# Four subtractions per weight block, on GpSimd instead of VectorE, in a decoder-block kernel that TensorE fills

## The chip, the cores and the metric

The kernel runs on one core of one Trainium2 chip. The core has a matrix engine (TensorE, in the profile PE, with its weight loads as PEld), a vector engine (VectorE, DVE), an activation engine (ScalarE, ACT), a general-purpose engine (GpSimd, POOL), an engine that only issues transfers here (SyncE, SP), and sixteen DMA engines. Each engine works through its own queue of instructions in order; semaphores tie the queues together. The metric is the device time in microseconds of one execution, of which the median over several runs is given.

## The reference: what is computed

One decoder layer on a sequence of 256 tokens with a model width of 2048, all in float32. Cut to its matrix products:

```python
proj = x @ w_in                      # 2048 -> q/k/v/gates of two attention branches, merge gates
...                                  # gated linear attention, forgetting attention
merged = sigmoid(ma) * (o @ w_branch_gla) + sigmoid(mb) * (of @ w_branch_fox)
x = layer_norm(ALPHA * x + merged @ w_out)
h = gelu(causal_dwconv(x @ w_gate)) * (x @ w_up)     # 2048 -> 5632, twice
x = layer_norm(ALPHA * x + h @ w_down)               # 5632 -> 2048
x = x + sigmoid(x @ w_ple_gate) * (p @ w_ple_proj)
```

The weights are read once each; nearly all the time goes into these products.

## The kernel before, in words

**Units of weights.** The weights lie in memory as a list of units, each 128 partitions by 2048 float32 (1 MB). Every unit is loaded by two transfers on SP's queue into two tiles `raw` of 128x1024, taken from a ring of five. TensorE multiplies in a rounded float32, so every operand is split in two: ScalarE writes the rounded value `hi` (a copy, line 113), VectorE the remainder `lo` = raw - hi (line 227 for plain units, line 195 for the units of this case). Both have rings of six tiles of 128x1024. A product is then three matmuls: hi by hi, lo by hi, hi by lo.

**Units with seven block products.** For `gv`, `gr`, `wo` and `dn` (the value projection, its output gate, the output projection and the down projection) a unit is a 2x2 set of blocks b11, b12, b21, b22 of 128x512. A plain ("classic") unit takes eight block products, 24 matmuls. In 33 chosen units (`s_units`) the Strassen-Winograd scheme takes seven, 21 matmuls, for which four differences of weight blocks are needed beside b11, b21 and b22:

t1 = b12 - b11, t3 = b12 - b22, t2 = b22 - t1, t4 = b21 - t2.

The function `differences` makes them in place, two per call. I call the four subtractions sub1 to sub4, in the order t1, t3, t2, t4. `prep_s` prepares such a unit: it splits b11 (tiles `hi_b`, `lo_b`), then b22 and b21 together, then overwrites b11 and b12 with t1 and t3 and splits these (`hi_t`, `lo_t`), then overwrites b22 and b21 with t2 and t4 and splits these. A subtraction that overwrites a block must come after the split that reads it: sub1 after the `lo_b` of b11, sub3 after the `lo_b` of b22 and b21. So a unit takes four `hi` and four `lo` tiles, in a chain that runs to and fro between ScalarE and VectorE. TensorE uses the seven products in a fixed order: b11, b21, b22 first, then t1, t3, t2, and t4 last (b11, t1, t3 and t2 accumulate in tiles named `dn_p`, `gv_p` and so on, the others in `dn`, `gv`).

**Parked units.** For 13 of the 33 units the differences are made long before, in an earlier stage (`park_gen`): the unit is loaded into a tile `td` of 128x2048, the four subtractions run, and GpSimd's queue stores the result to a DRAM tensor (line 165), from where `prep_s` reads it back. The other 20 subtract in the stage itself, on the tiles `raw`. Altogether there are 132 subtractions of 128x512, 52 on `td` and 80 on `raw`.

**What sets the order.** A function `unit` prepares three units ahead of the one in use (`ahead=3`); how far the preparation can really run ahead is set by the rings of `raw`, `hi` and `lo`. SP's queue is in the order of the program. The other queues are put in order by a scheduler that goes by priorities and expected costs when the kernel is built. In the stages `gv`, `gr`, `wo` and `dn` seven-product units mostly alternate with classic ones. GpSimd has little to do: it issues some accumulating loads (line 223), the stores of `td`, `sd` and others, and in the gate/up stage it copies two columns per block into `gp` for the convolution (line 1295), which VectorE's instructions of line 1302 read.

Of the kernel before, what the change touches and what calls it, by code (L numbers as in the profile page):

```python
# [14 lines left out]
ALU = mybir.AluOpType  # L15
# [58 lines left out]
def tile_block(ctx: ExitStack, tc: tile.TileContext, wu, wfv, wpp, xT_in, x_in, pT_in, wlr,  # L74
               chan, gnorm, lng, ident_in, mask_in, cmask_in, out):
    nc = tc.nc
# [69 lines left out]

    def differences(r0, r1, h):
        b12, b11, b22, b21 = r0[:, 0:512], r0[:, 512:1024], r1[:, 0:512], r1[:, 512:1024]
        sub = lambda o, a, b: nc.vector.tensor_tensor(o, a, b, ALU.subtract)  # L149
        if h == 0:  # L150
            sub(b11, b12, b11)
            sub(b12, b12, b22)
        else:
            sub(b22, b22, b11)
            sub(b21, b21, b22)

    def park_gen(units):

        for u, i in [(u, i) for u, i in parked.items() if u in units]:
            w = s8([P, 2048], name=f"td{i}")  # L160
            nc.sync.dma_start(w, wu[u])
            yield
            for h in range(2):
                differences(w[:, 0:1024], w[:, 1024:2048], h)
            nc.gpsimd.dma_start(td[i], w)
            yield

    def prep_s(u):
# [31 lines left out]
        if u not in parked:  # L200
            differences(r0, r1, 0)
        t3, t1_ = split(rt[0], "t13")
        if u not in parked:
            differences(r0, r1, 1)
# [240 lines left out]
    for u in range(8):  # L445
        hi, lo = fvu[u]
        for j in range(2):
            kt = 2 * u + j
            a = xT[kt // 4][:, kt % 4, :]
# [6 lines left out]
            for t, i, c in seq:  # L456
                o, n = fch[c]
# [1124 lines left out]
```

## Time and profile before

| | us |
|---|---|
| runs of the kernel before (three) | 1662.21, 1662.29, 1662.49 |
| profiled execution, first to last instruction (span) | 1660.7 |
| PE busy | 1654.7 |
| DVE busy | 1214.7 |
| ACT busy | 938.7 |
| POOL busy | 112.1 |

The profiled execution is known by its span; the median of the runs is 1.6 us above it, which is what lies before the first and after the last instruction. The page of the profile gives busy time per engine, the chain of work that ended last, and groups of instructions by line. Other views give the waits between engines, and the instructions of one engine in order of time. In that last view a row has the start, the duration, the engine, the line, the operation, the tiles written and read, their shapes, how many instructions were merged, and in brackets the idle time before it and what ended it. The durations of matmuls include their way through the pipeline; the pace is read from their starts.

### The profile page before, as it was taken

The numbers are of one execution on the slowest core, as the hardware profiler recorded it, in microseconds if no ns is written. First come the engines' busy times: TensorE is split into PE (matmuls) and PEld (weight loads), VectorE is DVE, ScalarE is ACT, GpSimd is POOL, SyncE is SP. The second block draws the span as 40 slices with busy tenths as digits, with TensorE's granted clock in tenths as the row PEclk, the third lists the DMA queues.
The fourth block names the chain that finished last, engine by engine and source line by source line (L and its number), as shares of the span: only waits on it lengthen the run. The fifth ranks groups of instructions, "written<-read, shape, count | busy, mean of one in ns | idle before, by whom it ended". The sixth has DMA issues, their size and how long they took to land.

```text
span 1660.7 us, 24379 instructions
## 1 busy us (share of the span) xinstructions
PE 1654.7 (100%) x8935; PEld 1438.0 (87%) x8935; DVE 1214.7 (73%) x1869; ACT 938.7 (57%) x1355; POOL 112.1 (7%) x262
## 2 busy tenths in 40 slices
PE   9999999999999999999999999999999999999999
PEld 8988888888888888888898888888888888888887
DVE  7644655678876547888987777877777787998774
ACT  6766666765555754455575445555545555556543
POOL 0111111100000110000010010000000000000000
PEclk9999999999999999999999999999999999999999
DMA  8799999986676997878856687777777668798554
GB/s 321 253 253 243 258 263 260 266 233 201 203 224 183 246 251 278 304 247 301 313 175 203 206 291 266 254 240 248 255 250 254 204 227 322 276 359 319 179 187 158
DMA packets 110313, 414.16 MB, mean 249 GB/s; under 512 B 12473, under 2 KB 13761, under 8 KB 104049
## 3 DMA queue, kind: packets, MB, share of 16 engines
q1 hardware_dynamic: 97584, 359.11, 62.7%
q0 software_dynamic: 12608, 53.49, 13.6%
q8 instruction: 70, 1.15, 0.3%
q14 instruction: 51, 0.41, 0.1%
HBM read 388.43 MB, written 24.13 MB: 248 GB/s over the span
## 4 chain that ended last, share of the span: by engine, by line
PE 98%; DMA 1%; DVE 0%; ACT 0%; POOL 0%; SPq 0%; issue 0%; POOLq 0%
PE dn L799 11%; PE psu L294 10%; PE psg L294 9%; PE psm L294 7%; PE pg L340 5%; PE psu L296 5%; PE psg L296 5%; PE gv L799 4%; PE wo L799 4%; PE psm L296 4%; PE psa L294 4%; PE dn_p L799 3%; PE gr L340 3%; PE fv L459 2%; PE gr L799 2%; PE psa L296 2%
## 5 line engine op out<-in xcount | busy, mean ns | idle before, releaser
L113 ACT ACTIVATE hi<-raw 128x1024 fp32r<-128x1024 f32 x502 | 528.2, 1057 | 405.1 <-issue 139.2
L227 DVE TENSOR_TENSOR lo<-raw,hi 128x1024 fp32r<-128x1024 f32 x444 | 539.7, 1222 | 214.9 <-ACT hi L113 210.8
L294 PE MATMUL psu<-x1T,hi 128*128 128x512 f32 x688 | 240.5, 392 | 0.0
L294 PE MATMUL psg<-x1T,hi 128*128 128x512 f32 x672 | 234.9, 392 | 0.0
L296 PE MATMUL psu<-x1T,lo 128*128 128x256 f32 x688 | 192.5, 280 | 0.0
L296 PE MATMUL psg<-x1T,lo 128*128 128x256 f32 x672 | 188.0, 280 | 0.0
L294 PE MATMUL psm<-xT,hi 128*128 128x512 f32 x512 | 181.2, 397 | 0.0
L294 PEld LDWEIGHTS psu<-x1T,hi 128*128 128x128 f32 x688 | 129.3, 188 | 27.4
L294 PEld LDWEIGHTS psg<-x1T,hi 128*128 128x128 f32 x672 | 126.2, 188 | 26.8
L296 PE MATMUL psm<-xT,lo 128*128 128x256 f32 x512 | 143.4, 280 | 0.0
L296 PEld LDWEIGHTS psu<-x1T,lo 128*128 128x128 f32 x688 | 130.7, 190 | 0.0
L296 PEld LDWEIGHTS psg<-x1T,lo 128*128 128x128 f32 x672 | 127.7, 190 | 0.0
L294 PEld LDWEIGHTS psm<-xT,hi 128*128 128x128 f32 x512 | 96.3, 188 | 19.6
L799 PE MATMUL dn<-hi,hC 128*128 128x512 f32 x400 | 111.4, 390 | 0.0
L296 PEld LDWEIGHTS psm<-xT,lo 128*128 128x128 f32 x512 | 97.3, 190 | 0.1
L294 PE MATMUL psa<-oT,hi 128*128 128x512 f32 x256 | 89.5, 392 | 0.0
L799 PEld LDWEIGHTS dn<-hi,hC 128*128 128x128 f32 x400 | 75.1, 188 | 15.5
L113 ACT ACTIVATE hi_t<-raw 128x1024 fp32r<-128x1024 f32 x40 | 42.5, 1062 | 65.7 <-DVE raw L149 51.1
L113 ACT ACTIVATE hi_b<-raw 128x512 fp32r<-128x512 f32 x66 | 55.2, 841 | 42.7 <-DMA raw<-in_wu_dram 19.9
L223 POOL DMA_DIRECT2D lo<-in_wu_dram x58 | 51.0, 879 | 320.9 <-ACT lo L113 125.6
L296 PE MATMUL psa<-oT,lo 128*128 128x256 f32 x256 | 71.6, 280 | 0.0
L195 DVE TENSOR_TENSOR lo_b<-raw,hi_b 128x512 fp32r<-128x512 f32 x66 | 62.5, 954 | 11.4 <-ACT hi_b L113 11.4
(374 smaller groups left out, 3254.5 us busy)
## 6 DMA issues: line engine op xcount, KB each, us to landing
raw<-in_wu_dram SPq DMA_DIRECT2D x555, 512.0 KB, 5.7
lo<-in_wu_dram POOLq DMA_DIRECT2D x58, 512.0 KB, 8.4
td<-in_wu_dram SPq DMA_DIRECT2D x13, 1024.0 KB, 8.6
td<-td POOLq DMA_DIRECT2D x13, 1024.0 KB, 6.7
td<-td SPq DMA_DIRECT2D x13, 1024.0 KB, 6.8
hS<-sd SPq DMA_DIRECT2D x19, 512.0 KB, 7.5
fvraw<-in_wfv_dram SPq DMA_DIRECT2D x13, 524.0 KB, 6.6
sd<-hs POOLq DMA_DIRECT2D x20, 256.0 KB, 5.5
```

The lines of the kernel that those rows point to most:

```text
L113: return nc.scalar.activation(o, i, AF.Copy, bias=0.0, scale=scale)
L195: nc.vector.tensor_tensor(lo, src, hi.bitcast(F32), ALU.subtract)
L223: nc.gpsimd.dma_start(lo, wu[u, :, 1024:2048], accum_op=ALU.add)
L227: i = nc.vector.tensor_tensor(lo, raw, hi.bitcast(F32), ALU.subtract)
L294: nc.tensor.matmul(ps, lhsT=hi[i // 8 if hoff == 0 else 0][:, w0 % 1024:w0 % 1024 + P], rhs=a[:, kt % 4, :], start=first and i == 0, stop= ...
L296: nc.tensor.matmul(ps[:, 256:512], lhsT=lo[i // 8 if hoff == 0 else 0][:, w0 % 1024:w0 % 1024 + P], rhs=a[:, kt % 4, 0:256], start=False, ...
L340: nc.tensor.matmul(bs[j][:, 0:m], lhsT=x, rhs=v[:, o:o + m], start=first and i == 0, stop=last and i == 2)
L459: nc.tensor.matmul(fbk[t][c][:, 0:n], lhsT=x, rhs=w[:, o:o + n], start=kt == 0 and i == 0, stop=kt == 15 and i == 2)
L799: nc.tensor.matmul(ps, lhsT=x, rhs=w, start=todo[id(ps)] == total[id(ps)], stop=todo[id(ps)] == 1)
```

## The change

The helper inside `differences` calls GpSimd instead of VectorE. All 132 subtractions move, those of the parked units and those of the others. Nothing else is edited; the order of the queues is made anew by the scheduler.

```diff
     def differences(r0, r1, h):
         b12, b11, b22, b21 = r0[:, 0:512], r0[:, 512:1024], r1[:, 0:512], r1[:, 512:1024]
-        sub = lambda o, a, b: nc.vector.tensor_tensor(o, a, b, ALU.subtract)
+        sub = lambda o, a, b: nc.gpsimd.tensor_tensor(o, a, b, ALU.subtract)
         if h == 0:
             sub(b11, b12, b11)
             sub(b12, b12, b22)
```

VectorE's queue in the down projection, at the second of two unparked units that follow each other (a classic unit between them), before. Names end in a number of the build; `raw_0` holds b12 and b11, `raw_1` holds b22 and b21:

```order
L195 TENSOR_TENSOR lo_b_13622<-raw_0_13615,hi_b_13621 128x512
L149 TENSOR_TENSOR raw_0_13615<-raw_0_13615 128x512
L195 TENSOR_TENSOR lo_b_13626<-raw_1_13616,hi_b_13625 128x1024
L149 TENSOR_TENSOR raw_0_13615<-raw_0_13615,raw_1_13616 128x512
L149 TENSOR_TENSOR raw_1_13616<-raw_1_13616,raw_0_13615 128x512
L149 TENSOR_TENSOR raw_1_13616<-raw_1_13616 128x512
L195 TENSOR_TENSOR lo_t_13632<-raw_0_13615,hi_t_13631 128x1024
L195 TENSOR_TENSOR lo_t_13638<-raw_1_13616,hi_t_13637 128x1024
L227 TENSOR_TENSOR lo_0_13666<-raw_0_13662,hi_0_13664 128x1024
L227 TENSOR_TENSOR lo_1_13672<-raw_1_13668,hi_1_13670 128x1024
L195 TENSOR_TENSOR lo_b_13707<-raw_0_13698,hi_b_13706 128x512
```

The same place on VectorE after:

```order
L195 TENSOR_TENSOR lo_b_13622<-raw_0_13615,hi_b_13621 128x512
L195 TENSOR_TENSOR lo_b_13626<-raw_1_13616,hi_b_13625 128x1024
L195 TENSOR_TENSOR lo_t_13632<-raw_0_13615,hi_t_13631 128x1024
L195 TENSOR_TENSOR lo_t_13638<-raw_1_13616,hi_t_13637 128x1024
L227 TENSOR_TENSOR lo_0_13666<-raw_0_13662,hi_0_13664 128x1024
L227 TENSOR_TENSOR lo_1_13672<-raw_1_13668,hi_1_13670 128x1024
L195 TENSOR_TENSOR lo_b_13707<-raw_0_13698,hi_b_13706 128x512
```

The six splits and their order stay; the four subtractions between them are gone. On GpSimd's queue, from the end of the gate/up stage into the down projection, there was before only this:

```order
L1295 COPY gp_13109<-gp_13109 128x1 x2
L1295 COPY gp_13218<-gp_13218 128x1 x2
L1295 COPY gp_13327<-gp_13327 128x1 x2
L1065 TENSOR_TENSOR mv<-mv,mhalf 128x1 x2
L1578 UNCONDITIONAL_BRANCH
```

And after (the rows of the down projection's first three unparked units; the next units follow in the same way):

```order
L149 TENSOR_TENSOR raw_0_13339<-raw_0_13339 128x512
L149 TENSOR_TENSOR raw_0_13339<-raw_0_13339,raw_1_13340 128x512
L149 TENSOR_TENSOR raw_1_13340<-raw_1_13340,raw_0_13339 128x512
L1295 COPY gp_13327<-gp_13327 128x1 x2
L149 TENSOR_TENSOR raw_1_13340<-raw_1_13340 128x512
L149 TENSOR_TENSOR raw_0_13532<-raw_0_13532 128x512
L149 TENSOR_TENSOR raw_0_13532<-raw_0_13532,raw_1_13533 128x512
L149 TENSOR_TENSOR raw_1_13533<-raw_1_13533,raw_0_13532 128x512
L149 TENSOR_TENSOR raw_1_13533<-raw_1_13533 128x512
L149 TENSOR_TENSOR raw_0_13615<-raw_0_13615 128x512
L149 TENSOR_TENSOR raw_0_13615<-raw_0_13615,raw_1_13616 128x512
L149 TENSOR_TENSOR raw_1_13616<-raw_1_13616,raw_0_13615 128x512
```

A queue that was empty through the down projection now has four subtractions for every unparked unit, sub1 to sub4 in that order. In the gate/up stage, GpSimd's queue around a parked unit, as one piece of the difference:

```order
 L1295 COPY gp_10709<-gp_10709 128x1 x2
 L1295 COPY gp_10819<-gp_10819 128x1 x2
+L149 TENSOR_TENSOR td_10883<-td_10883 128x512 x4
 L165 DMA td<-td_10883 128x2048
 L1295 COPY gp_10930<-gp_10930 128x1 x2
```

There the four subtractions stand between the column copies of two blocks, ahead of the store of `td`.

## The prediction

> **What bounds the kernel now.** I read the page's busy times and its chain first, then the waits of TensorE, to see whether anything but TensorE can shorten or lengthen the run.
>
> ```profile
> PE 1654.7 (100%) x8935; PEld 1438.0 (87%) x8935; DVE 1214.7 (73%) x1869; ACT 938.7 (57%) x1355; POOL 112.1 (7%) x262
> PE 98%; DMA 1%; DVE 0%; ACT 0%; POOL 0%; SPq 0%; issue 0%; POOLq 0%
> PE warm_ps L123 <- DVE warm L120: 1.2, 1, 1.2
> PE fv L459 <- ACT fvhi L113: 0.2, 1, 0.2
> ```
>
> TensorE is busy 1654.7 us, the chain that ended last is TensorE for 98%, and the only waits of TensorE on another engine are 1.2 and 0.2 us, both at the start. So relief for VectorE has nothing to buy: it ends no wait of TensorE. The change can be hidden, or it can open a wait that wasn't there. The question is therefore how far ahead of TensorE the preparation runs where the subtractions are, and how much of that lead the change uses up.
>
> **What is moved.** The subtractions of line 149, and the busy time of two stretches, a run of gate/up and a run of the down projection with two unparked units (start:end, length, then busy time and instructions of PE, PEld, DVE, ACT, POOL):
>
> ```profile
> L149 DVE TENSOR_TENSOR td<-td x52: 680/685/693, 633.2 to 1273.9; 128x512 f32<-128x512 f32 x52
> L149 DVE TENSOR_TENSOR raw<-raw x40: 678/691/694, 363.2 to 1510.2; 128x512 f32<-128x512 f32 x40
> L149 DVE TENSOR_TENSOR raw<-raw,raw x40: 678/691/694, 363.9 to 1509.5; 128x512 f32<-128x512 f32 x40
> 860.00:1325.00 465.00, 465.00 (x2687) 411.53 (x2686) 358.57 (x568) 238.01 (x361) 39.85 (x157) 1.00 0.72 245
> 1347.00:1368.00 21.00, 21.00 (x94) 17.43 (x93) 18.22 (x21) 11.43 (x12) 0.00 (x0) 1.00 0.58 199
> ```
>
> 52 x 0.685 + 80 x 0.691 = 91 us leave VectorE. In the down projection's stretch VectorE is busy 18.22 of 21 us; GpSimd does nothing there.
>
> **The price of one subtraction on GpSimd.** No row has this instruction there. The nearest:
>
> ```profile
> L284 POOL CAST mask<-maskf 128x1024 uint8<-128x1024 f32 x2 | 2.1, 1040 | 7.9 <-DMA maskf<-in_mask_dram 7.9
> L969 POOL TENSOR_TENSOR gst<-gst,mhalf 128x1 f32<-128x1 f32 x8 | 4.4, 555 | 161.6 <-DVE gst L967 161.6
> ```
>
> A copy with one input takes 1040 ns for 1024 elements, about 1.0 ns each. If two inputs cost no more than one, 512 elements cost 0.55 us; if each input is read by itself, 1.04 us; if the 555 ns of a two-input instruction with one element come on top, 1.6 us. I take 1.2 us, near the middle row-based value with part of the fixed cost, and keep 0.55 and 1.6 as the ends. [...]
>
> **Can both engines work at the same time?** Nearly all of VectorE's work in these stages has two inputs in SBUF. The rows where GpSimd reads SBUF meanwhile:
>
> ```profile
> 861.47 1.22 DVE L227 TENSOR_TENSOR lo<-raw,hi 128x1024 fp32r<-128x1024 f32 x1
> 861.62 1.24 POOL L1295 COPY gp<-gp 128x1 f32<-128x1 f32 x2 [13.20 <-DVE gp L323]
> L1295 POOL COPY gp<-gp x88: 178/185/1449, 861.6 to 1330.0; 128x1 f32<-128x1 f32 x88
> 830.56 0.74 DVE L1074 SCALAR_TENSOR_TENSOR z<-z,mv,lnb 128x512 f32<-128x512 f32 x1
> 830.73 0.99 POOL L1065 TENSOR_TENSOR mv<-mv,mhalf 128x1 f32<-128x1 f32 x1 [123.42 <-DVE mv L1064]
> ```
>
> Two copies of one column, median 185 ns each, take 1.24 us when they begin inside a VectorE instruction that ends at 862.69, and end right after it; the worst takes 1449 ns. The small GpSimd instruction of 830.73 takes 0.99 us instead of 0.55, again behind a VectorE instruction with two inputs that ends at 831.30. So GpSimd stands still while VectorE runs such an instruction. The other direction, VectorE held by a long GpSimd instruction, no run shown here has: GpSimd has no long one beside VectorE's. I take it to be held as well.
>
> [...]
>
> **The lead, and what a pair costs.** One period of the down projection, a seven-product unit and the classic one behind it:
>
> ```profile
> 1360.56 0.69 DVE L195 TENSOR_TENSOR lo_b<-raw,hi_b 128x512 fp32r<-128x512 f32 x1
> 1361.28 0.69 DVE L149 TENSOR_TENSOR raw<-raw 128x512 f32<-128x512 f32 x1
> 1361.89 1.22 DVE L195 TENSOR_TENSOR lo_b<-raw,hi_b 128x1024 fp32r<-128x1024 f32 x1
> 1363.03 1.41 DVE L149 TENSOR_TENSOR raw<-raw,raw 128x512 f32<-128x512 f32 x2
> 1364.47 0.69 DVE L149 TENSOR_TENSOR raw<-raw 128x512 f32<-128x512 f32 x1
> 1365.08 2.52 DVE L195 TENSOR_TENSOR lo_t<-raw,hi_t 128x1024 fp32r<-128x1024 f32 x2
> 1367.52 1.22 DVE L227 TENSOR_TENSOR lo<-raw,hi 128x1024 fp32r<-128x1024 f32 x1
> 1369.62 1.22 DVE L227 TENSOR_TENSOR lo<-raw,hi 128x1024 fp32r<-128x1024 f32 x1 [0.88 <-ACT hi L113]
> 1370.76 0.69 DVE L195 TENSOR_TENSOR lo_b<-raw,hi_b 128x512 fp32r<-128x512 f32 x1
> 1365.28 1.06 ACT L113 ACTIVATE hi_t<-raw 128x1024 fp32r<-128x1024 f32 x1 [0.39 <-DVE raw L149]
> 1370.32 0.39 PE L799 MATMUL dn_p<-hi_t,hS 128*128 128x512 f32 x1
> 1371.45 0.62 PE L799 MATMUL dn_p<-hi_t,hS 128*128 128x512 f32 x2
> 1373.04 0.62 PE L799 MATMUL dn<-hi,hC 128*128 128x512 f32 x2
> ```
>
> VectorE's period, from one short `lo_b` (1360.56) to the next (1370.76), is 10.2 us. That is TensorE's own time for 21 + 24 matmuls at a pitch of 0.227 us (five starts from 1370.32 to 1371.45), 45 x 0.227 = 10.2. The last `lo_t` (t2 and t4) is done at 1367.6; TensorE needs it from 1371.68, the second matmul of the row 1371.45. The lead is 4.1 us.
>
> Now the same period with subtractions of 1.2 us that exclude VectorE. From the end of the short `lo_b`, 1361.25: sub1 to 1362.45, the long `lo_b` 1363.7, sub2 1364.9, sub3 1366.1 (beside it ScalarE's `hi_t`, 1.06 us), first `lo_t` 1367.3, sub4 1368.5, then ScalarE's second `hi_t`, with nothing to run beside it, 1369.6, second `lo_t` 1370.8, the two `lo` of the classic unit and the next short `lo_b` 1373.85. The second `lo_t` is 3.2 us late, which the 4.1 us still hide. The next unit starts 2.4 us late (1373.85 against 1371.45): 12.6 us of work in a period of 10.2. A second unparked unit in a row is 2.4 + 3.2 - 4.1 = 1.5 us too late for TensorE, and a third would add 2.4 more. A parked unit has 10.2 - 6.8 = 3.4 us to spare (six splits, 0.69 + 5 x 1.22 = 6.8) and pays the debt back; so does a place where classic units follow each other.
>
> **The places.** I went through the 20 unparked units in order of time by their rows of `lo_b` and `lo_t`. In `gv` three stand in a row in each half, but the first of each starts 13.7 us or more ahead of the second, more than 12.6, so only the third stalls: 2 x 1.5 = 3.0 (the starts of the first and second are the first four rows below). In `gr` two, the first with 13.9 us: 0. In `wo` one, with 6.5 us of lead: 0. In the down projection's first half there are two places with two in a row: 1.5 for the first, and for the second, where the lead is only 1.6 and 2.6 us, about 2.4: 3.9. In the second half parked and unparked alternate, but the lead is 1.2 to 1.8 us at three units, which gives 0.9, 2.0 and 0.7: 3.6. The first and the last unit of the short leads are the last two rows; the second `lo_t` comes late there because it waits for its `hi_t`:
>
> ```profile
> 362.49 0.69 DVE L195 TENSOR_TENSOR lo_b<-raw,hi_b 128x512 fp32r<-128x512 f32 x1
> 378.82 0.69 DVE L195 TENSOR_TENSOR lo_b<-raw,hi_b 128x512 fp32r<-128x512 f32 x1
> 406.56 0.69 DVE L195 TENSOR_TENSOR lo_b<-raw,hi_b 128x512 fp32r<-128x512 f32 x1
> 420.30 0.68 DVE L195 TENSOR_TENSOR lo_b<-raw,hi_b 128x512 fp32r<-128x512 f32 x1
> 1491.30 1.23 DVE L195 TENSOR_TENSOR lo_t<-raw,hi_t 128x1024 fp32r<-128x1024 f32 x1 [1.21 <-ACT hi_t L113]
> 1512.10 1.23 DVE L195 TENSOR_TENSOR lo_t<-raw,hi_t 128x1024 fp32r<-128x1024 f32 x1 [1.21 <-ACT hi_t L113]
> ```
>
> Sum: 3.0 + 3.9 + 3.6 = 10.5 us.
>
> **What I cost at nothing.** The 52 subtractions on `td` in the branch and gate/up stages: there ScalarE waits for TensorE to free a tile, so the rings are full:
>
> ```profile
> 1110.45 1.06 ACT L113 ACTIVATE hi<-raw 128x1024 fp32r<-128x1024 f32 x1 [0.81 <-PE psu L294]
> raw<-in_wu_dram SPq DMA_DIRECT2D x555, 512.0 KB, 5.7
> ```
>
> A unit there takes 32 matmuls, by the row of that stage 465 / (2687 / 32) = 5.5 us. The tile freed at 1110.4 comes round after three units, 16.6 us, and less the 2.8 us of its own half unit it is wanted at 1124.2; its `lo` can be done 2.4 us after 1110.4. The lead is about 11 us.
>
> Four subtractions hold VectorE for at most 4.8 us per parked unit, in place of 2.7, and VectorE is busy 77% there. Behind them on GpSimd wait the column copies of the next block, and behind those VectorE's taps and the `lo` in its queue; that costs lead, and only what goes beyond some 11 us would reach TensorE. The store of `td` comes some microseconds later and is read back a stage later. The ring of `raw` comes free 1 to 3 us later and SP's loads with it; the first `lo_t` frees the next unit's second tile, which lands 5.7 us later (the second row), still before the `lo_b` that wants it. On the GpSimd queue of the down projection nothing else stands.
>
> The sum is made against the profiled execution, 1660.7 us; the median of the runs is 1.6 above that, so 1662.3 + 10.5 = 1673.
>
> **Rivals.** (1) VectorE isn't held: the subtractions run beside the splits. Then sub1 and sub2 end at 1363.7, where VectorE's sub2 ended before, sub4 at 1366.1 instead of 1365.16, and the second `lo_t` is 0.9 us late against a lead of 4.1 (1.2 at the shortest). Nothing stalls: 1662. It speaks for it that VectorE's being held is in no row, and against it that GpSimd's being held is. The same follows under exclusion if sub3 and sub4 run ahead of the first `lo_t` so that the second `hi_t` is hidden, and the subtraction is 0.8 us or less: 6.8 + 4 x 0.8 = 10.0, under the period. That is the point from which it decides. (2) The subtraction takes 1.6 us: a period of 14.2, 4 us lost per unparked unit in a row, and single ones stall too; by the same places some 30 us, 1692. The 555 ns for one element speak for it. (3) The parked units' subtractions starve behind VectorE in gate/up, the column copies wait, and the lead of 11 us is used up: 2 to 3 us at each of eight places, 20 us, 1682 with the forecast's term left at nothing; against it VectorE is idle 23% of that stage. (4) It gets faster: a wait on VectorE that hid in TensorE's busy time; the waits of TensorE speak against it.
>
> **Chances.** The forecast (held both ways, about 1.2 us) 0.58, its own range 1666 to 1681; (1) 0.27; (2) and (3) together 0.12; (4) 0.03. A difference under 0.2%, 3.3 us, can hardly be told from none. So faster 0.03, same 0.27, slower 0.70. The range takes in (1) at its lower end and leaves out the worst of (2): 1662 to 1688.
>
> **What the profile after would show.** Right: line 149 on POOL with a mean well above 1.2 us (it includes its waiting), VectorE's splits between them starting late with GpSimd named or with stretched durations, TensorE's first waits on VectorE's `lo_t` in `gv` and `dn`, none in gate/up. Wrong: no such waits, or waits at parked units' stages, at `gp`, or on the loads of `raw`.

## The result, and the profile after

The changed kernel takes 1687.6 us (median of three runs, 1686.28 to 1689.07) against 1662.29 before: a ratio of 1.0152, with a 95% interval from 1.0138 to 1.0167. It is 25.3 us slower. The forecast was 10.5 us slower, 1673, with a range of 1662 to 1688 and 1666 to 1681 for the forecast itself. The direction was right. The time lies just inside the wide range and outside the narrow one, and the size was 2.4 times what I had worked out. The profiled execution has a span of 1687.0 us, 26.3 more than that of before.

The profile page of the kernel after, busy time by engine and the chain that ended last:

```profile
PE 1666.5 (99%) x8935; PEld 1438.7 (85%) x8935; DVE 1192.4 (71%) x1737; ACT 935.4 (55%) x1355; POOL 328.6 (19%) x394
PE 78%; DMA 5%; POOL 5%; issue 5%; DVE 3%; ACT 2%; POOLq 0%; SPq 0%; DVEq 0%; ACTq 0%
```

Of the chain, TensorE held 98% before; it is 78% now, and the rest runs through GpSimd, transfers and VectorE. VectorE, from which 91 us were taken, is busy only 22 us less. The waits of TensorE after (in total, times, longest, us), without the one at the start that was there before:

```profile
PE dn_p L799 <- DVE lo_t L195: 4.5, 6, 0.9
PE dn_p L799 <- ACT hi_t L113: 3.3, 4, 0.8
PE psg L296 <- DVE lo L227: 2.6, 3, 0.9
PE gv_p L799 <- DVE lo_t L195: 2.3, 3, 0.8
```

Most of the waits are on `hi_t` and `lo_t`, in `gv` and `dn`, as forecast (the smaller groups, of 1.0 us and less, are left out here). Three more, on `lo` in the gate/up stage, were not. The subtractions after, by tile (duration as least/median/most, in ns), and the long `lo_b`, a group of VectorE's instructions that was stretched:

```profile
L149 POOL TENSOR_TENSOR td<-td x52: 1282/1358/2362, 633.0 to 1284.5; 128x512 f32<-128x512 f32 x52
L149 POOL TENSOR_TENSOR raw<-raw x40: 1280/2148/2208, 362.8 to 1534.8; 128x512 f32<-128x512 f32 x40
L149 POOL TENSOR_TENSOR raw<-raw,raw x40: 1282/1298/2163, 364.2 to 1533.4; 128x512 f32<-128x512 f32 x40
L195 DVE TENSOR_TENSOR lo_b<-raw,hi_b 128x1024 fp32r<-128x1024 f32 x33 | 46.9, 1422 | 14.0 <-ACT hi_b L113 13.9
```

A subtraction that meets nobody takes 1.28 us (0.69 on VectorE, 1.2 forecast). Those within one tile `raw` have a median of 2.15: 24 of the 40 begin while VectorE is in a split and end 1.14 to 1.16 us after it, and the wait is counted in their duration. The other direction, which no row of before showed, is there as well: the long `lo_b` takes 1422 ns in the mean, where its row before has 1.22 us.

This is one period of the down projection after, at an unparked unit behind an unparked one (VectorE, then GpSimd, ScalarE and TensorE):

```profile
1408.09 1.82 DVE L195 TENSOR_TENSOR lo_b<-raw,hi_b 128x512 fp32r<-128x512 f32 x2
1413.56 1.33 DVE L195 TENSOR_TENSOR lo_t<-raw,hi_t 128x1024 fp32r<-128x1024 f32 x1 [3.65 <-ACT hi_t L113]
1417.17 1.23 DVE L195 TENSOR_TENSOR lo_t<-raw,hi_t 128x1024 fp32r<-128x1024 f32 x1 [2.28 <-ACT hi_t L113]
...
1420.58 0.68 DVE L195 TENSOR_TENSOR lo_b<-raw,hi_b 128x512 fp32r<-128x512 f32 x1
1408.85 2.21 POOL L149 TENSOR_TENSOR raw<-raw 128x512 f32<-128x512 f32 x1 [5.30 <-DVE lo_b L195]
1411.14 2.67 POOL L149 TENSOR_TENSOR raw<-raw,raw 128x512 f32<-128x512 f32 x2
1413.89 2.16 POOL L149 TENSOR_TENSOR raw<-raw 128x512 f32<-128x512 f32 x1
1416.08 1.06 ACT L113 ACTIVATE hi_t<-raw 128x1024 fp32r<-128x1024 f32 x1 [2.55 <-POOL raw L149]
1417.19 0.50 PE L799 MATMUL dn_p<-hi_t,hS 128*128 128x512 f32 x1 [0.83 <-ACT hi_t L113]
1418.45 0.50 PE L799 MATMUL dn_p<-lo_t,hS 128*128 128x512 f32 x1 [0.76 <-DVE lo_t L195]
```

It comes to what the working of the prediction had, in nearly the same order. The long `lo_b` starts just ahead of the first subtraction here and ends at 1409.91; the subtraction waits for it inside its 2.21 us and ends 1.15 us later, at 1411.06. Then follow two subtractions, the first `lo_t`, the fourth subtraction, ScalarE alone, the second `lo_t`, the two `lo`. From one short `lo_b` (1408.09) to the next (1420.58) it is 12.5 us; 12.6 was forecast, and TensorE needs 10.2. VectorE is idle 3.65 and 2.28 us in it. So VectorE is not overloaded here: the engines take turns in a chain that has become too long.

I measured where the span grew from the first matmul of each stage to the first of the next, in both traces:

| stage | before, us | after, us | more | forecast |
|---|---|---|---|---|
| `gv` | 83.1 | 88.7 | 5.6 | 3.0 |
| `gr` to the second branch | 164.0 | 165.0 | 0.95 | 0 |
| branches | 133.1 | 133.1 | 0 | 0 |
| `wo` | 83.9 | 84.8 | 0.85 | 0 |
| gate/up | 497.3 | 500.7 | 3.4 | 0 |
| `dn` | 226.65 | 242.7 | 16.1 | 7.5 |

The remaining stages are 0.6 us shorter together, which gives the 26.3. The largest part, the down projection, in the view by stretches of time (start:end, length, then busy time and count of PE, PEld, DVE, ACT, POOL, granted clock, share of the DMA engines, GB/s), before:

```profile
1332.20:1558.80 226.60, 226.60 (x1002) 187.79 (x1001) 184.46 (x206) 125.15 (x135) 1.00 (x1) 1.00 0.81 295
```

and after:

```profile
1342.50:1585.00 242.50, 234.64 (x1001) 189.76 (x1000) 164.37 (x167) 123.55 (x135) 70.93 (x42) 0.98 0.76 275
```

TensorE, busy without a gap before, is idle 7.9 us in the stage by this view, its matmul records behind a wait are longer (0.50 us in the rows above, 0.39 else), and its granted clock is 0.98 in the mean. Counted by the starts of matmuls (over all stages), 24 starts come more than 0.25 us behind the pitch, 19.9 us in all, against 0.25 us before; 19 matmuls run at a granted clock of 0.50, 0.2 us more each, 3.8 us. Some 2.5 us lie in many small gaps, since the first matmul behind a wait starts its successor 0.34 us later, not 0.227.

### The profile page after: what moved, and what is told of

It is laid out like the page before. It is cut to its first block, busy times and chain, and to the rows that moved or that the text cites. A ratio compares the mean times of both kernels' runs of the same rounds, so it can differ in the third digit from the quotient of the medians.

```text
span 1687.0 us, 24463 instructions
## 1 busy us (share of the span) xinstructions
PE 1666.5 (99%) x8935; PEld 1438.7 (85%) x8935; DVE 1192.4 (71%) x1737; ACT 935.4 (55%) x1355; POOL 328.6 (19%) x394
## 3 DMA queue, kind: packets, MB, share of 16 engines
q8 instruction: 70, 1.15, 0.3%
## 4 chain that ended last, share of the span: by engine, by line
PE 78%; DMA 5%; POOL 5%; issue 5%; DVE 3%; ACT 2%; POOLq 0%; SPq 0%; DVEq 0%; ACTq 0%
PE psg L294 9%; PE psu L294 9%; PE psm L294 7%; POOL raw L149 5%; PE pg L340 5%; PE psg L296 5%; DMA raw<-in_wu_dram 5%; PE psu L296 4%; PE dn L799 4%; PE psm L296 3%; PE psa L294 3%; PE gr L340 3%; PE fv L459 2%; PE wo L799 2%; PE gr L799 2%
## 5 line engine op out<-in xcount | busy, mean ns | idle before, releaser
L227 DVE TENSOR_TENSOR lo<-raw,hi 128x1024 fp32r<-128x1024 f32 x444 | 555.7, 1261 | 201.6 <-ACT hi L113 198.1
L149 POOL TENSOR_TENSOR raw<-raw 128x512 f32<-128x512 f32 x40 | 73.2, 1830 | 234.4 <-DVE lo_b L195 191.2
L195 DVE TENSOR_TENSOR lo_t<-raw,hi_t 128x1024 fp32r<-128x1024 f32 x40 | 51.9, 1297 | 83.4 <-ACT hi_t L113 83.4
L149 POOL TENSOR_TENSOR td<-td 128x512 f32<-128x512 f32 x52 | 80.0, 1539 | 78.7 <-DMA td<-in_wu_dram 75.9
```

What stands on the lines that cost most here:

```text
L149: sub = lambda o, a, b: nc.gpsimd.tensor_tensor(o, a, b, ALU.subtract)
L195: nc.vector.tensor_tensor(lo, src, hi.bitcast(F32), ALU.subtract)
L227: i = nc.vector.tensor_tensor(lo, raw, hi.bitcast(F32), ALU.subtract)
```

## The experiments

For all of them the kernel before, run on the same chip, gave 1662.3 us. I call the time between the end of a unit's short `lo_b` and the first matmul of that unit its lead, and count the 33 units in order of time from 0.

**The parked units alone, and the others alone.** The helper takes the engine as an argument. In the first kernel the 52 subtractions on `td` go to GpSimd, in the second the 80 on `raw`:

```diff
-        sub = lambda o, a, b: nc.gpsimd.tensor_tensor(o, a, b, ALU.subtract)
+        sub = lambda o, a, b: eng.tensor_tensor(o, a, b, ALU.subtract)
```

> Only the 52 subtractions of the parked units run on GpSimd, the 80 on `raw` stay on VectorE. Theory A (the trace after: three stalls of about 1.0 us in gate/up at units whose lead was already 0.7 us, and nothing else from the parked units): 1665 to 1666 us. Theory B (the prediction's: the parked units are hidden, all of the loss comes from the 80): 1662 to 1663.

> Only the 80 subtractions on `raw` run on GpSimd, the 52 of the parked units stay on VectorE. Theory A: the rest of the loss, 1683 to 1685 us, with no stall in gate/up. Theory B: the whole of it, 1687. If the two parts worked on each other, e1 and e2 would not add up to the 25.3 us of the change.

Measured: 1665.72 us for the parked ones (ratio 1.0020, 1.0011 to 1.0030), +3.4, and 1683.88 for the others (1.0128, 1.0113 to 1.0143), +21.6. The sum, 25.0, is close to the change's 25.3: the two parts add up within the noise, except that the 0.85 us of `wo` are in neither of the two traces. The step that costed the `td` subtractions at nothing is wrong by 3.4 us, and the stall at the unparked units is twice the forecast. With the parked ones alone the list of TensorE's waits gains one entry, the one on `lo` in gate/up, 2.6 us in three times, word for word as in the list after the change; with the others alone it has only those in `gv` and `dn`.

**Does GpSimd's reading do it, or its being busy?** Each subtraction is replaced by two copies with one input on GpSimd, 0.61 us each (1.22 together, reading); or by three memsets, 0.525 + 0.525 + 0.30 (1.35 together, only writing); or by one copy:

```diff
-        sub = lambda o, a, b: nc.gpsimd.tensor_tensor(o, a, b, ALU.subtract)
+        sub = lambda o, a, b: [nc.gpsimd.tensor_copy(o, b if o is a else a) for _ in range(2)]
```
```diff
+        sub = lambda o, a, b: [nc.gpsimd.memset(o[:, 0:n], 0.01) for n in (512, 512, 256)]
```
```diff
+        sub = lambda o, a, b: nc.gpsimd.tensor_copy(o, b if o is a else a)
```

> Each of the 132 subtractions is replaced by two GpSimd copies of one 128x512 block, about 1.1 to 1.2 us together; the differences are not computed. GpSimd still reads SBUF. Theory A (VectorE's two-input instructions and GpSimd's reading instructions exclude each other, and that lengthens the period of a unit and the classic unit behind it from 10.2 to over 12): a period of about 12 us and most of the loss, 1677 to 1688. Theory C (the longer chain through GpSimd is the cause, whatever VectorE does beside it): the same time as e4.

> Each of the 132 subtractions is replaced by three GpSimd memsets (512, 512 and 256 columns of the block), about 1.2 us together; the differences are not computed. GpSimd writes SBUF and reads nothing. Theory A: VectorE isn't held and doesn't hold GpSimd, the period stays 10.2 us, 1662 to 1665. Theory C: the chain is as long as in e3, and so is the time, 1677 to 1688.

> Each of the 132 subtractions is replaced by one GpSimd copy of a 128x512 block (0.6 us, reads SBUF); the differences are not computed. The prediction's point of decision: below about 0.8 us the period of a unit and its classic neighbour stays under 10.2 us even when VectorE and GpSimd exclude each other (6.8 + 4 x 0.6 + 1.1 = 10.3 with a bare second rounding, 9.2 without). Theory A: 1662 to 1666. If any handing over to GpSimd costs TensorE time, whatever its length: above 1670.

Measured: two copies 1681.91 us (1.0117, 1.0102 to 1.0132), +19.6; memsets 1662.89 (1.0005, 0.9995 to 1.0014), +0.6; one copy 1662.47 (1.0002, 0.9992 to 1.0011), +0.2. Line 149 with two copies:

```profile
L149 POOL COPY raw<-raw x160: 611/617/1687, 363.2 to 1532.2; 128x512 f32<-128x512 f32 x160
```

Line 149 with memsets; the only wait of TensorE on another engine that is left there is the one of 1.2 us at the start:

```profile
L149 POOL MEMSET raw<- x240: 302/525/534, 354.0 to 1507.6; 128x512 f32 x79, 128x256 f32 x41
```

No memset takes longer than 534 ns, so none waited for VectorE; copies take up to 1687 ns. The two kernels don't keep GpSimd in the chain equally long, though. A memset reads nothing, so the three that stand for sub2 need only the load, and the scheduler put them ahead of the unit's chain. GpSimd behind the short `lo_b` of an unparked unit in the down projection, with memsets (and the second `lo_t` of that unit) and with two copies:

```profile
1360.81 3.88 POOL L149 MEMSET raw<- 128x512 f32 x9 [4.89 <-DVE lo_b L195]
1365.82 1.22 DVE L195 TENSOR_TENSOR lo_t<-raw,hi_t 128x1024 fp32r<-128x1024 f32 x1 [1.17 <-ACT hi_t L113]
1404.41 7.14 POOL L149 COPY raw<-raw 128x512 f32<-128x512 f32 x8 [5.28 <-DVE lo_b L195]
```

Nine memsets take 3.88 us. Eight copies would take 4.9 us if nothing held them (8 x 0.61) and take 7.14. So the memsets alone don't part reading from length. An estimate from these rows says how much length could do: with sub2's 1.35 us put back, the second `lo_t` would be done at 1368.4 instead of 1367.04, and TensorE's first matmul that reads it starts at 1371.46. A longer chain without exclusion would therefore have gone unseen at this unit; over many units no run shows it. What the runs do show is the exclusion itself: copies (611 ns at the least, up to 1687) and subtractions (1.28 us alone, 2.15 in the median of those within one tile `raw`) are stretched beside VectorE's splits and memsets (534 ns at most, 525 in the median) are not, and the time goes with it: +19.6 us with reads, +0.6 with writes. A subtraction that begins beside a split ends about its own length after it (1.15 us in the period shown above, 1.28 alone).

One copy per subtraction costs nothing (+0.2 us), although it reads too and is stretched too (on `raw` 614 ns in the median, up to 1626). The prediction's first rival had its point of decision there: 6.8 + 4 x 0.8 = 10.0 us is under the period of 10.2, and 0.61 is under 0.8. In the memset kernel the exclusion is missing, in the one-copy kernel the length, and TensorE has no wait in either beyond the 1.2 us at the start; the kernels that stall have both.

**Does a parked unit pay the debt back?** Eight of the 20 unparked units are on GpSimd, no two of them next to each other among the 33; all else is on VectorE:

```diff
+    moved = {sorted(s_units)[i] for i in (0, 3, 6, 8, 14, 16, 22, 24)}
...
-            differences(r0, r1, 0)
+            differences(r0, r1, 0, nc.gpsimd if u in moved else nc.vector)
```

> Only 8 of the 20 unparked units subtract on GpSimd, those that open a run or stand alone (the first of each half of `gv`, of `gr`, the one of `wo`, and four of `dn`); all others and the parked ones on VectorE. Theory A (a unit on GpSimd hands 2 to 3 us of delay to the next, and only the next one stalls TensorE; a neighbour on VectorE can absorb it): 1662 to 1664 us. Theory F (each unparked unit costs TensorE about the same, 21.6 us / 20): 1671.

Measured: 1665.50 us (1.0019, 1.0009 to 1.0029), +3.2, between what the two theories gave. There was no stall at units 16 and 17, nor in `gv`. But the lead that unit 16 used up did not come back. The short `lo_b` of units 17 and 18 (parked) start at 1360.56 and 1370.76 before, in rows that the prediction shows; that of unit 19, before:

```profile
1382.11 0.69 DVE L195 TENSOR_TENSOR lo_b<-raw,hi_b 128x512 fp32r<-128x512 f32 x1 [1.11 <-ACT hi_b L113]
```

and units 17, 18 and 19 with the eight units moved (line 195 is 196 there):

```profile
1363.37 0.69 DVE L196 TENSOR_TENSOR lo_b<-raw,hi_b 128x512 fp32r<-128x512 f32 x1
1372.60 0.68 DVE L196 TENSOR_TENSOR lo_b<-raw,hi_b 128x512 fp32r<-128x512 f32 x1
1384.68 0.69 DVE L196 TENSOR_TENSOR lo_b<-raw,hi_b 128x512 fp32r<-128x512 f32 x1 [2.07 <-ACT hi_b L113]
```

Against their first matmuls (1368.28, 1378.48, 1388.68 before; 1368.91, 1379.11, 1389.31 here) the leads were 7.0, 7.0 and 5.9, and are 4.9, 5.8 and 3.9. Unit 16's debt of 2.1 shrinks to 1.2 at unit 18 and is back at 1.9 at unit 19, where VectorE waits 2.07 us for a `hi_b` whose load came late. Units 17 to 20 have their subtractions on VectorE and make no debt of their own. The units moved later meet the shortened leads: unit 22 stalls TensorE by 1.0 us, and unit 25, behind moved unit 24, by 0.6.

**A sixth tile `raw`.** The debt stays, it seems, because the loads come later with it: a tile comes free later, and the next load cannot start. The room for a sixth tile is made by moving other tiles closer together:

```diff
-GAPS = (96, 64, 80)
+GAPS = (8, 8, 80)
-        return rlo.tile([P, 1152], F32R, tag="lo", name=f"lo{name}")[:, o:o + 1024]
+        return rlo.tile([P, 1040], F32R, tag="lo", name=f"lo{name}")[:, o:o + 1024]
-        r0, r1 = [ring.tile([P, 1024], F32, tag="raw", bufs=5, name=f"raw{u}_{h}")
+        r0, r1 = [ring.tile([P, 1024], F32, tag="raw", bufs=6, name=f"raw{u}_{h}")
```

> The change, with a ring of six `raw` tiles instead of five (room made by narrower `lo` tiles and two smaller unused gaps). Theory D (the debt isn't paid back because the next loads come late, since they wait for a tile of the ring): stalls at fewer units, 1674 to 1683 us. Theory E (only the exclusion of the two engines counts, the loads are early enough): within 1.5 us of 1687.6.

Measured: 1697.36 us (1.0212, 1.0197 to 1.0227), slower than the change itself, which no theory expected. The stalls counted by starts of matmuls had nevertheless fallen from 19.9 to 9.2 us. To part the two edits I ran the new layout with six tiles and the subtractions on VectorE, and the new layout with five tiles and the subtractions on GpSimd:

> The kernel before (subtractions on VectorE) with the memory layout of e7: six `raw` tiles, narrower `lo` tiles, smaller gaps. It tells whether e7's 1697 us come from the layout or from the change. Theory D (a sixth tile removes about half of the stalls, as e7's trace shows 9.2 us of them instead of 19.9, and the layout itself slows TensorE throughout): 1682 to 1687 us, so that the change costs 10 to 15 us in this layout. Theory E (the layout is neutral and six tiles make the change worse): 1662.

> The change in the layout of e7, but with five `raw` tiles. Theory D: slower than e7 by about 10 us, 1703 to 1710. Theory E: faster than e7 or the same.

Measured: 1686.61 us on VectorE (1.0147, 1.0130 to 1.0164) and 1703.01 with five tiles on GpSimd (1.0247, 1.0231 to 1.0262). The layout alone costs 24.3 us, without a single stall; more on that in the last section. Inside this layout, six tiles instead of five save 5.65 us (stalls of 9.2 instead of 15.3), and the change with six tiles costs 10.8 over the same layout without it. The short `lo_b` of unit 19, behind parked unit 18, and its first matmul, with five tiles:

```profile
1408.90 0.69 DVE L195 TENSOR_TENSOR lo_b<-raw,hi_b 128x512 fp32r<-128x512 f32 x1 [2.48 <-ACT hi_b L113]
1413.61 0.39 PE L799 MATMUL dn_p<-hi_b,hC 128*128 128x512 f32 x1
```

and with six:

```profile
1405.80 0.69 DVE L195 TENSOR_TENSOR lo_b<-raw,hi_b 128x512 fp32r<-128x512 f32 x1 [0.61 <-ACT hi_b L113]
1413.16 0.39 PE L799 MATMUL dn_p<-hi_b,hC 128*128 128x512 f32 x1
```

The lead is 4.0 us with five tiles, as it was at unit 18, and 6.7 with six: with a tile more, the parked unit does pay back. So the ring of five tiles is a part of the cause. It is not the whole of it, since 9.2 us of stalls remain. How large its part is in the layout of the changed kernel, no run shows: none has six tiles there.

**Is it the volume of the transfers?** The parked units read their differences back by a transfer of 1 MB on the same queue. Here half of it is read, and the half is used twice:

```diff
-            nc.sync.dma_start(w, td[parked[u]])
-            rt = (w[:, 0:1024], w[:, 1024:2048])
+            nc.sync.dma_start(w[:, 0:1024], td[parked[u], :, 0:1024])
+            rt = (w[:, 0:1024], w[:, 0:1024])
```

> The change, but a parked unit reads back only half of its differences (0.5 MB instead of 1 MB) and uses t1 and t3 in place of t2 and t4 too, so 13 x 0.5 MB less is loaded in `wo` and `dn`; that part of the result is not computed. Theory D': the DMA engines run at their full rate behind the stalls in `dn`, and that is what keeps a parked unit from paying the debt back: 1680 to 1685. Theory E: 1686 to 1689.

Measured: 1685.73 us (1.0143, 1.0127 to 1.0158), 1.9 less than the change, with intervals that overlap. 6.5 MB less to transfer change little. At unit 19, behind parked unit 18, the lead is 2.6 us in this run, where the change has 4.0: half the read-back did not bring the next load earlier. The volume is at most a small part.

**Which parked units cost 3.4 us?** The 52 subtractions on `td` on GpSimd, save those of the three early ones in gate/up; all on `raw` on VectorE:

```diff
+                differences(w[:, 0:1024], w[:, 1024:2048], h, nc.vector if i in (5, 6, 7) else nc.gpsimd)
```

> Parked units subtract on GpSimd except the three early ones in gate/up (their 12 subtractions stay on VectorE); all 80 on `raw` stay on VectorE. Theory A (e1's 3.4 us are the three stalls at units with a lead of 0.7 us): 1662 to 1663. If the other parked units cost something that shows as no wait: 1664 to 1666.

Measured: 1662.41 us (1.0001, 0.9992 to 1.0010). So those three units hold all the 3.4 us, and the other ten cost nothing. The place, after the change:

```profile
957.89 4.17 POOL L149 TENSOR_TENSOR td<-td 128x512 f32<-128x512 f32 x3
958.00 2.90 DVE L1302 SCALAR_TENSOR_TENSOR yc<-gp,chn,yc 128x256 f32<-128x256 f32 x2
960.82 4.59 DVE L227 TENSOR_TENSOR lo<-raw,hi 128x1024 fp32r<-128x1024 f32 x3
963.20 0.39 PE L296 MATMUL psg<-x1T,lo 128*128 128x256 f32 x1 [0.86 <-DVE lo L227]
```

and before:

```profile
949.67 0.38 ACT L113 ACTIVATE tmp<-psg 128x256 f32<-128x256 f32 x1 [3.73 <-PE psg L296]
949.95 1.05 ACT L113 ACTIVATE hi<-raw 128x1024 fp32r<-128x1024 f32 x1
953.34 1.22 DVE L227 TENSOR_TENSOR lo<-raw,hi 128x1024 fp32r<-128x1024 f32 x1
955.25 0.28 PE L296 MATMUL psg<-x1T,lo 128*128 128x256 f32 x1
```

Before, this `lo` was done at 954.56 and used at 955.25: a lead of 0.7 us, not 11. ScalarE made the `hi` for it only at 949.95, right behind a copy `tmp` that had waited 3.73 us for TensorE, so the lead was lost in ScalarE's queue. After, two taps of line 1302 take 2.90 us between GpSimd's subtractions (483 ns each in the mean before), and TensorE waits 0.86 us for the `lo` behind them. The same happens at 1008.7 and 1054.2.

No run was faster than the kernel before. Three equal it: with one copy, with memsets (both leave the differences out), and with ten parked units moved. They move work off an engine that TensorE was not waiting for.

## Why the prediction was right and wrong

**The mechanism of one pair and its unit prices were right.** TensorE bound the kernel, and relief for VectorE bought nothing. The subtraction takes 1.28 us (1.2 forecast, ends 0.55 and 1.6), and the period is 12.4 to 12.5 us (12.6). That VectorE is held as well, the open question between the forecast and the first rival, stood in no row of before; the forecast took it without one. The runs after show both directions: a subtraction that begins in a split ends 1.14 to 1.16 us after it, and the long `lo_b` takes 1422 ns in the mean, 1222 before. At unit 17, the second unparked in a row in `dn`, the stall is 1.3 us (1.5).

**The step that failed was "a parked unit has 3.4 us to spare and pays the debt back".** By it, debts end at the next parked unit, and each place in `dn` could be priced by itself. The stalls in `dn`, unit by unit:

| unit | forecast, us | measured, us |
|---|---|---|
| 17 | 1.5 | 1.3 |
| 19 and 20 | 2.4 | 4.45 |
| 25 | 0 | 3.6, and 2.4 from the clock |
| 27 | 0.9 | 0 |
| 29 | 2.0 | 0.5 |
| 31 | 0.7 | 2.3, and 1.6 from the clock |

Together these are the 16.1 us. They are one execution's: with the 80 alone on GpSimd, and no stretch at 0.50 in the stage up to unit 30, units 25, 27 and 29 cost 3.6, 1.5 and 1.5.

The 3.4 us count VectorE's work only. Parked unit 18 before, the issue of unit 19's loads on SP's queue and the first `hi` made from them:

```profile
1370.87 0.94 SPq L183 DMA_DIRECT2D raw<-in_wu_dram  x2
1381.45 0.63 ACT L113 ACTIVATE hi_b<-raw 128x512 fp32r<-128x512 f32 x1 [1.71 <-DMA raw<-in_wu_dram]
```

and after, with VectorE:

```profile
1385.96 0.97 SPq L183 DMA_DIRECT2D raw<-in_wu_dram  x2
1394.98 0.63 ACT L113 ACTIVATE hi_b<-raw 128x512 fp32r<-128x512 f32 x1 [3.02 <-DMA raw<-in_wu_dram]
1395.65 0.69 DVE L195 TENSOR_TENSOR lo_b<-raw,hi_b 128x512 fp32r<-128x512 f32 x1 [2.43 <-ACT hi_b L113]
```

VectorE has its time to spare, and stands idle in it for 2.43 us, because the next unit's load lands late. It lands late because it is issued late, and not because it takes longer: from issue to `hi_b` it is 10.6 us before and 9.0 after, but the issue comes 7.6 us ahead of unit 18's first matmul before (1378.48) and only 4.1 ahead after (1390.10). In SP's queue these loads stand behind the classic unit's loads of line 217, and the first of those goes out as unit 17's second `lo_t` ends and frees its tile: at 1367.70 before (that `lo_t` ends at 1367.60), at 1383.37 after (1383.35). So a late chain also makes its own next loads late. Unit 19 starts with a lead of 4.0 us (1396.34 to 1400.30) where it had 5.9 before, and units 19 and 20 cost 2.0 us more than forecast. I had seen this ("The ring of `raw` comes free 1 to 3 us later and SP's loads with it") and costed it at nothing, because the load still came before the `lo_b` that wants it in the schedule of before. The eight moved units and the sixth tile show the step as wrong.

**Unit 25 was left out of the sum.** The prediction says that in the second half of `dn` parked and unparked units alternate. They do from unit 25 on; but units 24 and 25 are both unparked. The second `lo_t` of unit 25 and the matmul that first reads it, before:

```profile
1461.21 1.23 DVE L195 TENSOR_TENSOR lo_t<-raw,hi_t 128x1024 fp32r<-128x1024 f32 x1 [0.60 <-ACT hi_t L113]
1464.38 0.39 PE L799 MATMUL dn_p<-lo_t,hS 128*128 128x512 f32 x1
```

That is a lead of 1.9 us, or 1.7 as the prediction counts it (to the `hi_t` matmul at 1464.16), as short as at the three units that it priced. By its own rule unit 25 owed 3.2 - 1.7 = 1.5 us. The rest of its 3.6 us is open: other work of VectorE, adds and statistics of the layer norm, lies between units 24 and 25 as well, and no run took that apart from the debt. A smaller slip: the row of 1491.30 is the second of the three units with a short lead, not the first.

**In `gv`** I let only the third unit of each half stall, by 1.5 us each. The stalls are 1.0 at unit 2 and 0.4, 1.4 and 2.0 at units 3 to 5. The second half's first unit began with a lead of 6.8 us, not 10.6: again a debt that was carried on instead of being paid.

**"The rings are full", read from one row, was wrong at three places.** The lead of about 11 us in gate/up came from the row at 1110.45. It holds there, and the other ten parked units cost nothing; at three places the lead was 0.7 us. So the term that was put at nothing was worth 3.4 us. The third rival's path (subtractions, taps, `lo`) is what happens there, at three places for 0.9 to 1.1 us each, instead of eight for 2 to 3. The second rival's price, 1.6 us per subtraction, did not come. Its time, 1692, was nearer than my own, for another reason.

**A granted clock of 0.50 was not foreseen.** The waits themselves cost some 20 us; the granted clock added 3.8.

## What to carry to other kernels

When work moves to a second engine of a chain, price the chain's period against the bound engine's period, as was done here; but then carry the debt on from unit to unit, loads included, until a row shows it repaid, because spare time on one engine didn't repay here what waited for a buffer of a ring. A lead must be read at each place where it is used, at the shortest one above all, and not from one row in a long stage. Beside a VectorE that streams two-input work, GpSimd cost nothing in these runs when it wrote without reading (+0.6 us with the memsets), or when both engines' parts together still fitted into the period (+0.2 with one copy); it gained nothing either, since TensorE bound the kernel.

## What the hardware showed beyond that

**The granted clock was 0.50 behind two bunches of waits.** The changed kernel at unit 25, in the view by stretches (the last three numbers are the granted clock, the share of the DMA engines and GB/s):

```profile
1482.50:1489.30 6.80, 6.25 (x14) 4.57 (x15) 6.80 (x7) 5.75 (x7) 0.00 (x0) 0.50 0.70 233
```

The matmuls there (start, duration; in brackets the wait):

```profile
1480.18 0.50 PE L799 MATMUL dn_p<-lo_t,hS 128*128 128x512 f32 x1 [0.87 <-DVE lo_t L195]
1482.41 0.71 PE L799 MATMUL dn_p<-hi_t,hS 128*128 128x512 f32 x1 [0.81 <-ACT hi_t L113]
1483.67 0.79 PE L799 MATMUL dn_p<-lo_t,hS 128*128 128x512 f32 x1 [0.55 <-DVE lo_t L195]
1484.26 0.63 PE L799 MATMUL dn_p<-hi_t,hS 128*128 128x512 f32 x1
1484.69 0.63 PE L799 MATMUL dn<-hi_t,hC 128*128 128x512 f32 x1
```

Three waits lie within 4.4 us (1479.31 to 1483.67). From the second of them on the granted clock is 0.50 for 6.8 us (1.00 in the 7.5 us ahead of that), and matmuls start 0.43 us apart instead of 0.227: twelve of them here. At unit 31, behind two waits, it is 0.50 for 3.3 us (1540.6 to 1543.9), with seven such matmuls. The pair of waits in the period shown in the first section, 0.83 and 0.76 us, brought no such stretch, and neither did three waits of 0.83, 0.78 and 0.76 us at unit 25 in the kernel with two copies (matmuls at 1476.12, 1478.36 and 1479.61 there, granted clock 1.00 from 1470 to 1486). The longest wait in the bunches is 0.87 us. No run shows what sets a bunch with such a stretch behind it apart from one without.

**With the tiles closer together TensorE took 10.49 us for 45 matmuls, not 10.20.** The dearest group of matmuls of the down projection before (total, mean ns, idle):

```profile
L799 PE MATMUL dn<-hi,hC 128*128 128x512 f32 x400 | 111.4, 390 | 0.0
```

and in the closer layout with six tiles, with the subtractions on VectorE and then on GpSimd:

```profile
L799 PE MATMUL dn<-hi,hC 128*128 128x512 f32 x400 | 114.0, 396 | 0.0
L799 PE MATMUL dn<-hi,hC 128*128 128x512 f32 x400 | 113.8, 396 | 0.0
```

With six tiles and VectorE, TensorE has no wait that it didn't have before, and the run takes 24.3 us longer. From the first matmul of unit 19 to that of unit 20 it is 10.49 us there (1406.45 to 1416.94) and 10.20 before (1388.68 to 1398.88), 45 matmuls each. With five tiles and GpSimd the run is 40.7 us longer than before, of which 15.3 are stalls: an estimate of 25.4 for the layout there, beside 24.3 with six, so the number of tiles isn't what slows it. Which of the others does, the gaps or the tile width, no run here took apart.
